# The third gate and up tile of a SwiGLU feed-forward, as two full products or as seven block products

## The chip, the core and the metric

The kernel runs on one core of a Trainium2 chip. The metric is the device time of one execution in microseconds (us), the median of several. Five engines run their own instruction queues side by side and wait for each other by semaphores: TensorE (PE; its weight loads are shown as PEld), VectorE (DVE), ScalarE (ACT), GpSimd (POOL) and SyncE (SP), which here issues the DMA transfers. Every engine takes its instructions in the order in which the program lists them.

## The reference

Two layers of an encoder trunk on a sequence of 512 positions with model width 1024, in float32. Each layer is a half-step feed-forward, a token mixing (windowed attention beside dilated attention), and a second half-step feed-forward. Only the feed-forward matters here:

```
h = modulate(rmsnorm(x, norm), shift, scale)
gate, up = split(h @ wi, 2)          # wi: 1024 x 5632, so 2 x 22 tiles of 128 columns
x = x + 0.5 * g * ((silu(gate) * up) @ wo)
```

There are four feed-forwards, two per layer. The columns of `wi` are taken as 22 pairs of tiles, f0 to f21: the gate tile f and the up tile f, 128 columns each.

## The kernel before, in words

**Tiles and splitting.** Activations lie transposed: 128 features on the partitions, 512 positions along the row, eight such tiles (k = 0 to 7) for the 1024 features. TensorE multiplies in a format that keeps fewer bits than float32, so each operand is split into a high part (rounded by ACT) and a low part (the rest, subtracted by DVE), and each product is three matmuls: high by high, low by high, high by low (`mm3`, L224 to L228; `prod`, L485 to L490).

**A full tile.** A flat gate or up tile of 128 columns is eight k, three matmuls each, of 512 positions: 24 matmuls of 128x512. A pair f made flat is 48 of them (L573 to L581). Its two weights are loaded and split by `emit_chunk` (L139): for each weight an ACT copy `hi` and a DVE subtraction `lo` (L157, L158).

**A pair by block products.** In three of the four feed-forwards (all but the first one of layer 0, `wino = l + sub > 0`, L441), a pair f may be made in one go by the seven products of Strassen's scheme in its Winograd form (`pair`, L475): the two weights of 1024 rows by 128 columns side by side are a 2 by 2 matrix of blocks, the activation is cut at feature 512 and at position 256 into four blocks, and seven products of blocks with four k each stand in for eight. That is 7 x 4 x 3 = 84 matmuls of 128x256. Which pairs are made so is told by

```
def paired(l, sub, f):                       # L105
    return l + sub > 0 and f >= PLAIN        # PLAIN = 3, L25
flat = 2 * min(n, max(0, PLAIN - f0)) if wino else 2 * n     # L572: tiles of this third that stay flat
```

The weights' side of it is `emit_pair` (L164): besides the splits it forms sums and differences of weight blocks. On DVE these are four operations of 128x512 (L191, L193, L198, L200: `ta` and `raw`), three low parts of 128x1024 and one of 128x512 (L188: three `lo` and `l4`); on ACT the high parts (L185, L199).

The activations' side is `sums(k)` (L452), once per feed-forward for k = 0 to 3: on DVE four sums of halves of `t` (L457 to L460), on ACT one high part `sh` of 128x1024 (L463), on DVE one low part `sl` of 128x1024 (L464). Every pair by block products reads all four `sh` and `sl`.

**The order of a feed-forward.** The 22 pairs go in thirds of 7, 7 and 8. The first third starts with `group` (L371): four flat tiles (gate and up of f0 and f1), each in two halves of 256 positions, since the norm of the second half of the positions comes later. Behind each of the four tiles, `sums(k)` is called for one k (L567), `take` (L552) makes the SwiGLU product of a finished gate and up (silu L559 on ACT, product L560 on DVE, split L471 and L472), and `ahead` (L217) emits the next weights. Then come the flat tiles that are left (before: f2), then the block products (before: f3 to f6), then the output tiles of this third (`out_tiles`, L403). `ahead` emits a block pair early only when at most one flat weight is waiting; further pairs are emitted piece by piece inside `pair` (the generator `more`, advanced by `conv`, L498).

**What sets the order on an engine.** The program is recorded in this order, and a scheduler then lists the instructions of each engine with its own costs for each; the list is fixed when the program is built. So the place of an instruction in its engine's list can move by more than the code shows.

The three feed-forwards with block products are called A (second of layer 0), B (first of layer 1) and C (second of layer 1) below.

Of the kernel before, what the change touches and what calls it, by code (L numbers as in the profile page):

```python
# [21 lines left out]
HS = 256  # L22
NF = 22
THIRDS = ((0, 7), (7, 7), (14, 8))
PLAIN = 3  # L25
EPS = 1e-6
TWO_PI = 6.283185307179586
PI_2 = 1.5707963267948966
# [40 lines left out]
def tile_trunk(ctx: ExitStack, tc: tile.TileContext, xT, c, positions, adaT, cols, sink, wi1, wo1,  # L69
# [35 lines left out]
    def paired(l, sub, f):  # L105
        return l + sub > 0 and f >= PLAIN

# [330 lines left out]
    def ffn(l, sub, norm, pool, step, start=None, final=None, mod=None):  # L438
# [109 lines left out]
        for ti, (f0, n) in enumerate(THIRDS):  # L548
# [15 lines left out]
            if ti == 0:  # L564
                for p in (start() if start else group(norm, gs, sh, 4)):
# [4 lines left out]
                    if start:  # L570
                        step()
            flat = 2 * min(n, max(0, PLAIN - f0)) if wino else 2 * n  # L572
            for _ in range(done, flat):  # L573
# [618 lines left out]
```

## Time and profile before

| | us |
|---|---|
| median of 3 runs | 1941.79 (1940.43 to 1943.55) |
| profiled execution, its own time | 1941.13 |
| span of that execution, first to last instruction | 1939.4 |
| PE busy | 1903.8 (98%) |
| DVE busy | 1516.0 (78%) |
| ACT busy | 941.6 (49%) |
| PE on the chain that ended last | 90% |
| mean granted clock of TensorE | 0.994 |

Matmuls overlap in the records: one of 128x256 is shown with 0.28 us, but the next one may start 0.12 us after it. What a stretch of matmuls takes is therefore read from start to start. The same holds on DVE and ACT, where an operation's record reaches some hundredths of a microsecond into the next one.

### The profile page before, as it was taken

How to read it: one execution, taken by the hardware profiler on the slowest of the kernel's cores; microseconds unless marked ns; L12 is line 12 of the kernel's file. 1: busy time of each engine (PE TensorE's matmuls, PEld its weight loads, DVE VectorE, ACT ScalarE, POOL GpSimd, SP SyncE). 2: the span in 40 equal slices, each digit the busy share in tenths (PEclk: the TensorE clock that was granted, in tenths of full speed). 3: DMA queues.
4: the chain of work that ended last, by engine and by line, in shares of the span. 5: the costliest groups of instructions: out<-in, count | busy, mean ns of one | idle time of the engine just before them, and what ended most of it. 6: DMA issues, size and time to landing. Idle time of an engine off the chain costs nothing.

```text
span 1939.4 us, 30969 instructions
## 1 busy us (share of the span) xinstructions
PE 1903.8 (98%) x12000; PEld 1711.2 (88%) x12000; DVE 1516.0 (78%) x2653; ACT 941.6 (49%) x1782; POOL 85.5 (4%) x63
## 2 busy tenths in 40 slices
PE   7999999999999999999999999999999999999998
PEld 5788888898778999989999898999887799898998
DVE  8967484477888989899688898867778889686873
ACT  5422222246675554536445363644567656363552
POOL 2000000011210000000000000000211000000000
PEclk8999999999999999999999999999999999999999
DMA  8778384245422255464424545342543113233231
GB/s 298 282 255 308 126 304 137 76 129 139 118 55 66 77 164 195 142 209 129 142 66 152 196 144 161 109 131 83 153 116 99 44 57 111 86 106 123 87 110 44
DMA packets 84677, 267.95 MB, mean 138 GB/s; under 512 B 10673, under 2 KB 13361, under 8 KB 84530
## 3 DMA queue, kind: packets, MB, share of 16 engines
q1 hardware_dynamic: 84530, 265.98, 42.6%
q8 instruction: 94, 1.54, 0.3%
q14 instruction: 53, 0.43, 0.1%
HBM read 244.97 MB, written 2.10 MB: 127 GB/s over the span
## 4 chain that ended last, share of the span: by engine, by line
PE 90%; DVE 5%; ACT 2%; DMA 2%; issue 1%; SPq 0%; POOL 0%; DVEq 0%; ACTq 0%; POOLq 0%
PE mm L226 17%; PE mm L227 17%; PE mm L228 17%; PE mm L488 10%; PE mm L489 10%; PE mm L490 10%; PE ptr L732 2%; PE po L739 1%; PE po L740 1%; PE s L698 1%; PE s L699 1%; DVE araw L320 1%; DMA araw<-in_adaT_dram 1%; PE mm L661 1%; PE mm L663 1%
## 5 line engine op out<-in xcount | busy, mean ns | idle before, releaser
L157 ACT ACTIVATE hi<-raw 128x512 fp32r<-128x512 f32 (+5 forms) x253 | 215.7, 866 | 310.2 <-PE mm L228 224.2
L158 DVE TENSOR_TENSOR lo<-raw,hi 128x512 fp32r<-128x512 f32 (+5 forms) x253 | 259.2, 1037 | 88.6 <-ACT hi L157 87.6
L226 PE MATMUL mm<-hh,hi 128*128 128x512 f32 (+1 forms) x864 | 307.7, 357 | 6.9 <-ACT hh L298 6.6
L228 PE MATMUL mm<-hl,hi 128*128 128x512 f32 (+1 forms) x864 | 303.1, 355 | 2.8 <-DVE hl L299 2.8
L227 PE MATMUL mm<-hh,lo 128*128 128x512 f32 (+1 forms) x864 | 305.8, 355 | 0.0
L227 PE MATMUL mm<-gh,lo 128*128 128x512 f32 (+1 forms) x832 | 297.0, 357 | 0.0
L226 PE MATMUL mm<-gh,hi 128*128 128x512 f32 (+1 forms) x832 | 296.8, 357 | 0.0
L228 PE MATMUL mm<-gl,hi 128*128 128x512 f32 (+1 forms) x832 | 296.5, 356 | 0.0
L488 PE MATMUL mm<-sh,hi 128*128 128x256 f32 x912 | 260.0, 285 | 0.3 <-ACT sc L518 0.3
L489 PE MATMUL mm<-sh,lo 128*128 128x256 f32 x912 | 258.1, 283 | 0.0
L490 PE MATMUL mm<-sl,hi 128*128 128x256 f32 x912 | 258.0, 283 | 0.0
L185 ACT ACTIVATE hi<-raw 128x512 fp32r<-128x512 f32 x228 | 132.0, 623 | 140.3 <-issue 73.6
L396 DVE SCALAR_TENSOR_TENSOR x<-mm,fin,x 128x512 f32<-128x512 f32 (+1 forms) x156 | 101.4, 653 | 115.7 <-PE mm L228 115.2
L226 PEld LDWEIGHTS mm<-hh,hi 128*128 128x128 f32 x864 | 164.6, 191 | 29.7 <-ACT hh L298 8.1
L228 PEld LDWEIGHTS mm<-hl,hi 128*128 128x128 f32 x864 | 163.2, 190 | 25.9 <-DVE hl L299 4.7
L227 PEld LDWEIGHTS mm<-hh,lo 128*128 128x128 f32 x864 | 164.4, 190 | 20.7 <-DVE lo L1004 0.3
L228 PEld LDWEIGHTS mm<-gl,hi 128*128 128x128 f32 x832 | 157.2, 189 | 22.7
L227 PEld LDWEIGHTS mm<-gh,lo 128*128 128x128 f32 x832 | 157.2, 189 | 22.3
L226 PEld LDWEIGHTS mm<-gh,hi 128*128 128x128 f32 x832 | 157.2, 189 | 22.2
L488 PEld LDWEIGHTS mm<-sh,hi 128*128 128x128 f32 x912 | 174.0, 191 | 0.7 <-ACT sc L518 0.6
L489 PEld LDWEIGHTS mm<-sh,lo 128*128 128x128 f32 x912 | 174.2, 191 | 0.0
L490 PEld LDWEIGHTS mm<-sl,hi 128*128 128x128 f32 x912 | 174.1, 191 | 0.0
(185 smaller groups left out, 4017.1 us busy)
## 6 DMA issues: line engine op xcount, KB each, us to landing
raw<-in_wi_dram SPq DMA_DIRECT2D x171, 512.0 KB, 3.7
araw<-in_adaT_dram SPq DMA_DIRECT2D x144, 512.0 KB, 4.6
raw<-in_wo_dram SPq DMA_DIRECT2D x64, 448.0 KB, 3.8
raw<-in_wo_dram SPq DMA_DIRECT2D x32, 512.0 KB, 3.6
raw<-in_wqk_dram SPq DMA_DIRECT2D x26, 512.0 KB, 3.7
raw<-in_w_out_dram SPq DMA_DIRECT2D x16, 512.0 KB, 3.7
kh<-qh SPq DMA_DIRECT2D x40, 128.0 KB, 2.3
kl<-t SPq DMA_DIRECT2D x40, 128.0 KB, 2.3
```

What stands on the lines that cost most here:

```text
L157: A.activation(hi[:, sl], raw[:, sl], AF.Copy)
L158: V.tensor_tensor(lo[:, sl], raw[:, sl], hi.bitcast(F32)[:, sl], op=ALU.subtract)
L185: A.activation(d, r, AF.Copy)
L226: T.matmul(ps, wh, X[0][:, s], start=start, stop=False)
L227: T.matmul(ps, wl, X[0][:, s], start=False, stop=False)
L228: T.matmul(ps, wh, X[1][:, s], start=False, stop=stop)
L320: return V.tensor_tensor_reduce(out=raw, in0=raw, in1=by, scale=1.0, scalar=0.0, op0=ALU.mult, op1=ALU.add, accum_out=mod[:, l, ch, k:k + ...
L396: ins = V.scalar_tensor_tensor(x[:, m, s], ps[:, s], gate[:, m:m + 1], x[:, m, s], op0=ALU.mult, op1=ALU.add).ins
L488: T.matmul(ps, wh, xh, start=start and k == 0, stop=False, skip_group_check=True)
L489: T.matmul(ps, wl, xh, start=False, stop=False, skip_group_check=True)
L490: T.matmul(ps, wh, xl, start=False, stop=stop and k == 3, skip_group_check=True)
L732: T.transpose(p[:, j * 128:j * 128 + 128], self.sm[qt][:, c0:c0 + 128], ident)
```

## The change

`PLAIN` goes from 3 to 2, so in A, B and C the pair f2, the first one behind `group`, is made by block products too. Nothing else in the code is touched.

```diff
 THIRDS = ((0, 7), (7, 7), (14, 8))
-PLAIN = 3
+PLAIN = 2
```

In A, B and C each, 48 matmuls of 128x512 are gone and 84 of 128x256 are new. The weights of f2 go through `emit_pair` instead of twice `emit_chunk`: the same two transfers of 512 KB, four DVE subtractions of 128x512 less, and the eight DVE operations of a block pair more. The product and the split of a finished f2 (L560, L472) become the five DVE operations L524, L530, L532, L540 and L544.

On DVE, in A, this is what stands behind the last sum of k = 0 (L460) before the change, up to the last sum of k = 1 (L460 again); `lo<-raw,hi` at L158 is the low part of f2's two flat weights, `sl` the low part of the sums:

```order
L460 SCALAR_TENSOR_TENSOR sf<-t,fin,sf 128x256
L158 TENSOR_TENSOR lo<-raw,hi 128x512 x4
L464 TENSOR_TENSOR sl<-sf,sh 128x1024
L457 SCALAR_TENSOR_TENSOR sf<-t,both 128x256
L459 TENSOR_TENSOR sf<-t 128x256
L458 SCALAR_TENSOR_TENSOR sf<-t,fin,sf 128x256
L560 TENSOR_TENSOR sg<-sg,mm 128x512
L460 SCALAR_TENSOR_TENSOR sf<-t,fin,sf 128x256
```

And with the change, from the same instruction to the first sum of k = 1; the rows between are the block pair f2's weights, with `sl` of k = 0 among them:

```order
L460 SCALAR_TENSOR_TENSOR sf<-t,fin,sf 128x256
L191 TENSOR_TENSOR ta<-raw 128x512
L188 TENSOR_TENSOR lo<-raw,hi 128x1024
L193 TENSOR_TENSOR ta<-ta,raw 128x512
L464 TENSOR_TENSOR sl<-sf,sh 128x1024
L198 TENSOR_TENSOR raw<-raw,ta 128x512
L200 TENSOR_TENSOR raw<-raw 128x512
L188 TENSOR_TENSOR lo<-ta,hi 128x1024
L188 TENSOR_TENSOR l_6116<-raw,h_6115 128x512
L188 TENSOR_TENSOR lo<-raw,hi 128x1024
L457 SCALAR_TENSOR_TENSOR sf<-t,both 128x256
```

The sums of k = 1, 2 and 3 stand behind the whole weight work of f2. In A and C the list from L457 of k = 1 to the last `sl` is the same as before, word for word. In B two of the weight operations (`L191` and the first `lo`) stand some rows earlier, where three of the four `lo` of the flat f2 stood before; the other six stand behind L460 as here.

On PE, in A, this is the last of f2's flat matmuls before the change, and the first of f3's block products behind it:

```order
L226 MATMUL mm_6286<-hh7_5828,hi_6113 128x512
L227 MATMUL mm_6286<-hh7_5828,lo_6114 128x512
L228 MATMUL mm_6286<-hl7_5829,hi_6113 128x512
L488 MATMUL mm_6318<-hh4_5822,hi_6262 128x256
L489 MATMUL mm_6318<-hh4_5822,lo_6265 128x256
```

With the change, f2's block products follow `group` at once. Two of its seven products (24 matmuls) read the plain activations `hh`, `hl`; then come the rows below, with `sh_6100`, `sh_6161`, `sh_6201` the sums of k = 0, 1, 2, `sl_...` their low parts, and `mm_6371` already belonging to f3:

```order
L490 MATMUL mm_6245<-hl3_5821,hi_6108 128x256
L488 MATMUL mm_6246<-sh_6100,hi_6109 128x256
L489 MATMUL mm_6246<-sh_6100,lo_6112 128x256
L490 MATMUL mm_6246<-sl_6101,hi_6109 128x256
L488 MATMUL mm_6371<-hh4_5822,hi_6265 128x256
L488 MATMUL mm_6246<-sh_6161,hi_6109 128x256
L489 MATMUL mm_6246<-sh_6161,lo_6112 128x256
L490 MATMUL mm_6246<-sl_6162,hi_6109 128x256
L488 MATMUL mm_6246<-sh_6201,hi_6109 128x256
L489 MATMUL mm_6246<-sh_6201,lo_6112 128x256
L490 MATMUL mm_6246<-sl_6202,hi_6109 128x256
```

So the first readers of the sums have moved from behind the flat f2 to the 25th matmul behind `group`. The first reader of k = 3's low part (`sl_6235`) is the 49th matmul behind `group`; what stands ahead of it are f2's first two products, its sums of k = 0 to 2 in two products, four matmuls of `sh` of k = 3, and two early matmuls of f3. B and C have the same list on PE but for one matmul's place.

## Rows read from the trace of the kernel before

**Rows 1.** The page, busy time of each engine: share of the span, instructions.

```profile
PE 1903.8 (98%) x12000; PEld 1711.2 (88%) x12000; DVE 1516.0 (78%) x2653; ACT 941.6 (49%) x1782; POOL 85.5 (4%) x63
```

**Rows 2.** Waits of PE, whole run: total us, times, longest us.

```profile
PE mm L488 <- ACT sc L518: 0.3, 1, 0.3
```

**Rows 3.** Timeline of PE in A: start us, us, instruction.

```profile
661.54 0.40 PE L226 MATMUL mm<-hh,hi 128*128 128x512 f32 x1
...
672.44 0.28 PE L488 MATMUL mm<-hh,hi 128*128 128x256 f32 x1
...
682.52 0.28 PE L488 MATMUL mm<-hh,hi 128*128 128x256 f32 x1
```

**Rows 4.** Timeline of DVE in A, behind the first sums.

```profile
652.98 0.49 DVE L460 SCALAR_TENSOR_TENSOR sf<-t,fin,sf 128x256 f32<-128x256 f32 x1
653.38 2.50 DVE L158 TENSOR_TENSOR lo<-raw,hi 128x512 fp32r<-128x512 f32 x4
655.79 1.23 DVE L464 TENSOR_TENSOR sl<-sf,sh 128x1024 fp32r<-128x1024 f32 x1
656.92 0.48 DVE L457 SCALAR_TENSOR_TENSOR sf<-t,both 128x256 f32<-128x256 f32 x1
657.32 0.42 DVE L459 TENSOR_TENSOR sf<-t 128x256 f32<-128x256 f32 x1
657.65 0.49 DVE L458 SCALAR_TENSOR_TENSOR sf<-t,fin,sf 128x256 f32<-128x256 f32 x1
...
660.00 0.69 DVE L472 TENSOR_TENSOR gl<-sg,gh 128x512 fp32r<-128x512 f32 x1 [0.47 <-ACT gh L471]
...
667.34 1.23 DVE L464 TENSOR_TENSOR sl<-sf,sh 128x1024 fp32r<-128x1024 f32 x1
```

**Rows 5.** Timeline of DVE in A, the weights of a block pair.

```profile
668.49 0.69 DVE L193 TENSOR_TENSOR ta<-ta,raw 128x512 f32<-128x512 f32 x1
669.09 1.22 DVE L188 TENSOR_TENSOR lo<-raw,hi 128x1024 fp32r<-128x1024 f32 x1
670.22 0.69 DVE L200 TENSOR_TENSOR raw<-raw 128x512 f32<-128x512 f32 x1
```

**Rows 6.** Timeline of ACT in A: the silu of f1's gate.

```profile
658.86 0.60 ACT L559 ACTIVATE sg<-mm 128x512 f32<-128x512 f32 x1 [2.94 <-PE mm L228]
```

**Rows 7.** Timeline of DVE in B, behind the first sums.

```profile
1001.76 0.48 DVE L460 SCALAR_TENSOR_TENSOR sf<-t,fin,sf 128x256 f32<-128x256 f32 x1
1002.15 0.69 DVE L158 TENSOR_TENSOR lo<-raw,hi 128x512 fp32r<-128x512 f32 x1
```

**Rows 8.** Timeline of PE in B, the first matmul of the flat f2.

```profile
1010.07 0.40 PE L226 MATMUL mm<-hh,hi 128*128 128x512 f32 x1
```

**Rows 9.** Timeline of DVE in C, behind the first sums.

```profile
1595.54 2.50 DVE L158 TENSOR_TENSOR lo<-raw,hi 128x512 fp32r<-128x512 f32 x4
```

**Rows 10.** Timeline of PE in C, the first matmul of the flat f2.

```profile
1603.69 0.40 PE L226 MATMUL mm<-hh,hi 128*128 128x512 f32 x1
```

**Rows 11.** Timeline of PE behind a wait, elsewhere.

```profile
613.71 0.50 PE L226 MATMUL mm<-yah,hi 128*128 128x512 f32 x1 [1.72 <-ACT yah L801]
614.05 0.40 PE L227 MATMUL mm<-yah,lo 128*128 128x512 f32 x1
```

**Rows 12.** Windows with PE: stretch, length, PE busy (matmuls), granted clock, DMA share, GB/s.

```profile
13.00:14.00 1.00, 0.28 (x2) 1.00 1.05 345
16.00:17.00 1.00, 0.20 (x2) 0.71 0.99 406
26.00:27.00 1.00, 1.00 (x5) 0.67 1.04 401
46.00:54.00 8.00, 5.40 (x23) 1.00 0.92 351
611.00:614.00 3.00, 1.28 (x8) 1.00 0.25 97
```

**Rows 13.** Windows with all engines, end of B's first third: PE, PEld, DVE, ACT, POOL.

```profile
1051.00:1061.00 10.00, 10.00 (x86) 10.00 (x85) 6.69 (x10) 5.15 (x8) 0.00 (x0) 1.00 0.76 242
```

## The prediction

> **What bounds the kernel now.** I read the page first: PE is busy 98% of the span and DVE 78% [rows 1]. An average over stages decides nothing, so the waits of PE came next. The block products (L488 to L490) wait once in the whole run, for 0.3 us [rows 2]: in A, B and C PE never stands still behind `group`, and its own matmuls set the time there. The timeline of PE gives their price. In A the flat f2 begins at 661.54 and f3's block products at 672.44, f4's at 682.52 [rows 3]: a flat pair takes 10.90 us (48 matmuls, 0.227 each), a block pair 10.08 us (84 matmuls, 0.120 each). The timeline of DVE at the same place shows what PE's timeline hides. From 652.98 on DVE works through the sums with hardly a gap, and the low part of the last one (L464 of k = 3) ends at 667.34 + 1.23 = 668.57 [rows 4], which is 7 us after `group` has ended on PE. Nobody waits for it today, since PE has the flat f2 to do until 672.44. The flat pair is the cover under which the sums are made, and the change takes it away.
>
> **The change, part by part.**
>
> *Fewer columns on PE.* In each of A, B and C, 10.90 us of flat matmuls give way to 10.08 us of block products: -0.82 us, three times -2.5 us. The rows price a matmul of 256 columns at 0.120 us, more than half of 0.227. The Trainium skill (TensorE: Matmul & The Clock Gate, "Wait — 56ns, not 53.3ns?") gives a start-to-start time of the columns at 2.4 GHz plus about 2.5 ns, which makes 0.109 and 0.216 us, and a gain of 1.2 us for each of the three. The trace has dearer matmuls [rows 3], so it decides; by the page's figures the sum would come out 1.1 us lower.
>
> *More work on DVE ahead of the sums, in A.* Behind the sums of k = 0 stand today the four low parts of the flat f2, from 653.38 to 655.79 = 2.41 us [rows 4]. In their place come f2's eight weight operations: five of 128x512 at 0.60 us (669.09 - 668.49) and three of 128x1024 at 1.13 us (670.22 - 669.09) [rows 5], together 6.4 us, or 4.0 us more. One of them, the third low part, needs a high part that ACT makes only behind the silu of f1's gate, which waits for PE until 658.86 and takes 0.60 [rows 6]; with 0.6 us for the copy itself (my estimate, as long as the silu of the same size) it is there at 660.0, where DVE would have begun at 659.8: 0.2 us more. So L457 of k = 1, at 656.92 today [rows 4], comes at about 661.1. From there on DVE's list is today's word for word, and today it holds one gap, 0.47 us at 660.00 for ACT [rows 4], of which I drop 0.4, since f1's silu no longer stands in its way. The last low part then ends at 668.57 + 4.2 - 0.4 = 672.3.
>
> *Earlier need on PE, in A.* f2's block products begin at 661.54 in place of its flat ones. The first 24 matmuls read what is long there. The 49th is the first to read the low part of k = 3, and without a wait it would start at 661.54 + 48 x 0.120 = 667.3. It can't before 672.3: 5.0 us of waiting, spread over the chain k = 1 to 3. By the same sum DVE and ACT give the low part of k = 1 at 665.9 (0.8 us late), the high part of k = 2 at 667.7 (1.6 more), its low part at 669.5 (1.5 more), the rest before the last one. A resumed PE also loses something: behind a wait its second matmul came 0.34 us after the first, where 0.227 is the pace [rows 11], so 0.1 us; the restarts ahead of the 49th matmul lie inside the 5.0 us, three at or behind it (the last part of k = 3, f3's first weights, a copy by ACT) add 0.3. Together +5.3 us. PE is strictly in order, and the two matmuls of f3 that stand among these rows are too few to fill anything.
>
> *Not given back.* Queued behind PE's waits is all that follows in the feed-forward; as PE waited for nothing there [rows 2], a late start of f4 is a late end. f4 starts at 661.54 + 168 x 0.120 + 5.3 = 687.0 against 682.52 [rows 3]: +4.5 us in A.
>
> *C* repeats A: its DVE list is at the same operation at 1595.54 [rows 9], 942.16 us after A's 653.38, and PE at its flat f2 at 1603.69 [rows 10], 942.15 after 661.54. +4.5 us.
>
> *B* is milder. Three of f2's four flat low parts stand earlier in the list and make room there for two of the weight operations, so that six are left behind the first sums, with the low part of k = 0 among them. From 1002.15 [rows 7] these are four operations at 0.60 (three before that low part, one behind) and three of 1.13: 5.8 us, and L457 of k = 1 begins at 1007.95. From there to the end of the last low part it is as in A 11.2 us (672.3 - 661.1): 1019.15. PE begins f2 at 1010.07 [rows 8] and would be at its 49th matmul at 1015.83. Wait 3.3 us, 0.3 behind it, less 0.8: +2.8 us.
>
> *What lies beside other work.* DVE has some 5 us more to do in each first third (6.4 - 2.4 for the weights, about 1.3 for five combining operations in place of two). By the third's end it has room: in B from 1051 to 1061 it was busy 6.69 of 10 us while PE was full [rows 13]. Without that room it would cost up to 5 us each time; I take nothing. ACT, POOL and the two transfers of 512 KB are the same work at almost the same place, and the few transfers that change places on SP lie where PE waits for none.
>
> *Sum.* 4.5 + 2.8 + 4.5 = +11.8 us on the profiled execution's 1941.13 us: 1952.9. The median of the runs shown lies 0.7 us higher, so 1953.
>
> **The rivals.**
>
> *The products pay, the sums are in time.* PE takes its 0.82 us in each feed-forward and waits no more than today: 1941.8 - 2.5 = 1939.3, not slower. For it speaks that the block pairs wait for nothing now [rows 2]. It would need the last low part 4.2 us earlier than I have it in A, at about 668.1: from there the wait eats less than 0.82. Against it speaks that DVE runs without a gap from before the weight operations to the last low part, so nothing can bring it forward, and that its list is fixed.
>
> *Half of it is given back.* If PE's later pairs have hidden waits of other kinds, or DVE's list moves on faster than its neighbours suggest, the waits shrink to 2 to 3 us each: 1944 to 1949. Only the 0.3 us of [rows 2] is there to be given back, and the durations in the rows repeat to a hundredth.
>
> *TensorE's clock falls in the gaps.* At the start of the run PE was busy 0.28 us from 13 to 14 us, then hardly at all, and the granted clock went from 1.00 to 0.71 in the microsecond from 16 and came back in the one from 26 [rows 12]: some 10 us at 1.2 in place of 2.4 GHz. In A and C, PE will do only six matmuls between 664.9 and 669.5, in four pieces. If that is too little, up to 8 us of block products behind the gaps run at half speed and cost 4 us each in A and C: 1961. Against it: from 46 to 54 us PE was busy 5.4 of 8 us and the clock stayed at 1.00, and so it did around the wait of 1.72 us [rows 11], from 611 to 614 [rows 12]. The Trainium skill (TensorE: Matmul & The Clock Gate, "What's actually happening") says that the throttled state is the default and activity releases it; by that rule the gaps are a risk, and the first two of [rows 12] agree, but nothing in this trace shows gaps as dense as these.
>
> **How the numbers follow.** My forecast, all waits as computed and full clock: 78%, 1953, of its own range 1950 to 1956, since the unknown terms are small: the restarts (0 to 0.6 each time), the 0.4 and 0.2 us around ACT, and B's start. The clock: 12%, 1957 to 1965. Half given back: 6%. No wait: 4%. For 8 in 10 the range is 1949 to 1960: it holds my forecast's range, all but the top of the clock's and the edge of the third case. A measurement of this kernel tells about 0.2%, or 3.9 us, from no change. The forecast, the clock and most of the half are slower by more: 0.94. The case without waits lies at -0.13%, inside: it and the low end of the half make 0.04. A faster run would need more than all three savings: 0.02.
>
> **What would show it.** In the profile after, PE's waits must have new rows for L488 on ACT's `sh` (L463) and L490 on DVE's `sl` (L464), together some 3 to 4 us in each of A and C and 2 to 3 in B (the records of 0.28 us hide 0.16 of each wait), and hardly a row for f4 and later. The last L464 in A ends near 672.3 with DVE gapless ahead of it, f4's first matmul starts near 687.0, and 168 matmuls of 256 columns lie between `group`'s end and there. I am wrong if these waits are missing, if the distance from `group`'s end to f4 in A is under 22 us, if the granted clock falls below 1 there, or if DVE falls behind in the third's output tiles, which would add waits of L226 there.

## The result, and the profile after

The changed kernel takes 1960.64 us (median of four runs, 1957.55 to 1962.84) against 1942.28 us in the same job (1940.43 to 1943.55): ratio 1.0090, 95% interval 1.0073 to 1.0107, slower by 14 to 21 us. The forecast was 1953, the range 1949 to 1960. The median lies 0.6 us above the range; taken by the ratio from 1941.79, where the forecast started, it is 1959.3, inside by 0.7. The direction and the waits came as forecast; the size is larger, and TensorE's clock, which the forecast took as full, has a part in it. The profiled execution took 1958.53 us, 17.4 more than before's, and its span is 1956.4 us, 17.0 more.

The page, busy time by engine, answers to [rows 1]:

```profile
PE 1910.4 (98%) x12108; PEld 1720.2 (88%) x12108; DVE 1532.9 (78%) x2674; ACT 949.9 (49%) x1800; POOL 85.6 (4%) x63
```

PE's share has not moved. An average shows nothing of a loss of 17 us that sits in three places. The waits of PE (total us, times, longest us) show it; against [rows 2] the block products have two new rows, 9.2 us in eight waits:

```profile
PE mm L490 <- DVE sl L464: 5.1, 5, 1.3
PE mm L488 <- ACT sh L463: 4.1, 3, 1.4
PE mm L488 <- ACT sc L518: 0.2, 1, 0.2
```

The timeline of PE in A, from the first matmul of f2 (`group`'s end, as it is called below) to the first of f4, answers to [rows 3]:

```profile
664.10 0.28 PE L488 MATMUL mm<-hh,hi 128*128 128x256 f32 x1
...
667.58 0.28 PE L489 MATMUL mm<-sh,lo 128*128 128x256 f32 x1
668.50 0.39 PE L490 MATMUL mm<-sl,hi 128*128 128x256 f32 x1 [0.64 <-DVE sl L464]
670.32 0.39 PE L488 MATMUL mm<-sh,hi 128*128 128x256 f32 x1 [1.43 <-ACT sh L463]
670.55 0.28 PE L489 MATMUL mm<-sh,lo 128*128 128x256 f32 x1
672.09 0.58 PE L490 MATMUL mm<-sl,hi 128*128 128x256 f32 x1 [1.27 <-DVE sl L464]
672.57 0.58 PE L488 MATMUL mm<-sh,hi 128*128 128x256 f32 x1
...
673.38 0.41 PE L488 MATMUL mm<-sh,hi 128*128 128x256 f32 x1
673.59 0.41 PE L489 MATMUL mm<-sh,lo 128*128 128x256 f32 x1
...
675.50 0.28 PE L490 MATMUL mm<-sl,hi 128*128 128x256 f32 x1
...
690.12 0.28 PE L488 MATMUL mm<-hh,hi 128*128 128x256 f32 x1
```

Three gaps stand ahead of the low part of k = 1 and of the high and the low part of k = 2. From start to start they lose 0.8, 1.7 and 1.4 us, where the working had 0.8, 1.6 and 1.5. The line at 675.50 is the 49th matmul, the first to read the low part of k = 3; the fourth wait of the working, ahead of it, is not there. Behind the third gap the matmuls follow each other at 0.21 us and not at 0.120. The windows with PE (stretch, length, PE busy, granted clock, DMA share, GB/s) say why:

```profile
670.00:671.00 1.00, 0.50 (x2) 1.00 0.00 0
671.00:672.00 1.00, 0.00 (x0) 0.90 0.00 0
672.00:673.00 1.00, 0.91 (x3) 0.50 0.00 0
674.00:675.00 1.00, 1.00 (x7) 0.50 0.08 16
675.00:676.00 1.00, 1.00 (x10) 0.90 0.32 33
676.00:677.00 1.00, 1.00 (x11) 1.00 0.82 246
```

PE had begun three matmuls since 667.7 when the granted clock went to 0.50 (1.2 GHz) at 671.8; it came back at 675.2. The same happened in C, not in B. The third rival of the prediction, which had 12%, is part of the answer.

DVE's last low part in A answers to [rows 4], where it ended 7.03 us behind `group`'s end (668.57 - 661.54). Here it ends 673.56 + 1.23 - 664.10 = 10.69 us behind it; the forecast said 672.3 - 661.54 = 10.76. The 49th matmul starts 11.40 us behind `group`'s end, so PE, at half clock, came 0.7 us later than the operand that it was to wait for.

```profile
673.56 1.23 DVE L464 TENSOR_TENSOR sl<-sf,sh 128x1024 fp32r<-128x1024 f32 x1
```

One measure serves for all that follows: the distance from `group`'s end to f4's first matmul, read from PE's timeline in each phase of each profile. A phase that starts late for another reason does not change it. "Lows" are low parts of the sums. Us:

| kernel | A | B | C | sum, over before's 63.0 | runs, ratio to before [95%] |
|---|---|---|---|---|---|
| before | 20.98 | 21.06 | 20.98 | 0 | 1 |
| forecast for the change | 25.5 | 23.9 | 25.5 | +11.8 | 1.0058 |
| changed | 26.02 | 24.36 | 26.37 | +13.7 | 1.0090 [1.0073, 1.0107] |
| e1 changed, again | 27.19 | 24.38 | 27.14 | +15.7 | 1.0090 [1.0076, 1.0104] |
| e2 only B changed | 20.98 | 25.26 | 20.98 | +4.2 | 1.0023 [1.0015, 1.0032] |
| e3 before, two lows more | 20.98 | 20.98 | 20.98 | -0.1 | 0.9997 [0.9988, 1.0006] |
| e4 changed, two lows more | 28.49 | 27.37 | 28.70 | +21.5 | 1.0129 [1.0114, 1.0145] |
| e5 changed, sums ahead | 22.96 | 22.16 | 22.98 | +5.1 | 1.0034 [1.0021, 1.0046] |
| e6 e5 and two lows on GpSimd | 26.14 | 24.31 | 26.09 | +13.5 | 1.0084 [1.0072, 1.0097] |
| e7 changed, waits filled | 25.45 | 25.26 | 25.47 | +13.2 | 1.0082 [1.0068, 1.0096] |
| e8 before, f3 flat too | 21.79 | 21.79 | 21.79 | +2.4 | 1.0020 [1.0011, 1.0028] |
| e9 before, again | 20.98 | 21.06 | 20.98 | 0 | 1.0004 [0.9995, 1.0013] |
| e10 before, start edited | 20.98 | 21.06 | 20.98 | 0 | 0.9986 [0.9977, 0.9995] |
| e11 changed, start edited | 27.48 | 25.09 | 27.26 | +16.8 | 1.0077 [1.0063, 1.0091] |

Of the first profile's 17.0 us, 13.7 lie in the three phases. Most of the rest (2.6 us) was lost before A began: `group` ended at 664.10 against 661.54, in a part of the program that the change does not touch: up to 600 us the instructions in the two traces are, engine by engine, the same in the same order.

### The profile page after: what moved, and what is told of

Same layout as the page of the kernel before. It is cut to its first block, busy times and chain, and to the rows that moved or that the text cites. A ratio compares the mean times of both kernels' runs of the same rounds, so it can differ in the third digit from the quotient of the medians.

```text
span 1956.4 us, 31234 instructions
## 1 busy us (share of the span) xinstructions
PE 1910.4 (98%) x12108; PEld 1720.2 (88%) x12108; DVE 1532.9 (78%) x2674; ACT 949.9 (49%) x1800; POOL 85.6 (4%) x63
## 4 chain that ended last, share of the span: by engine, by line
PE 87%; DVE 6%; ACT 2%; DMA 2%; issue 1%; POOL 0%; SPq 0%; DVEq 0%; ACTq 0%; POOLq 0%
PE mm L226 16%; PE mm L228 16%; PE mm L227 16%; PE mm L488 10%; PE mm L490 10%; PE mm L489 10%; PE ptr L732 2%; PE po L739 1%; PE po L740 1%; PE s L698 1%; DMA araw<-in_adaT_dram 1%; PE s L699 1%; PE mm L661 1%; PE mm L663 1%; PE mm L662 1%
## 5 line engine op out<-in xcount | busy, mean ns | idle before, releaser
L157 ACT ACTIVATE hi<-raw 128x1024 fp32r<-128x1024 f32 (+5 forms) x241 | 208.3, 878 | 309.4 <-PE mm L228 222.8
L158 DVE TENSOR_TENSOR lo<-raw,hi 128x1024 fp32r<-128x1024 f32 (+5 forms) x241 | 251.3, 1053 | 85.6 <-ACT hi L157 84.4
L226 PE MATMUL mm<-hh,hi 128*128 128x512 f32 (+1 forms) x816 | 289.7, 356 | 8.2 <-ACT hh L298 8.2
L227 PE MATMUL mm<-hh,lo 128*128 128x512 f32 (+1 forms) x816 | 288.1, 354 | 0.0
L228 PE MATMUL mm<-hl,hi 128*128 128x512 f32 (+1 forms) x816 | 284.8, 354 | 1.7 <-DVE hl L299 1.7
L488 PE MATMUL mm<-sh,hi 128*128 128x256 f32 x960 | 275.7, 287 | 4.5 <-ACT sh L463 4.1
L490 PE MATMUL mm<-sl,hi 128*128 128x256 f32 x960 | 273.2, 285 | 5.2 <-DVE sl L464 5.1
L489 PE MATMUL mm<-sh,lo 128*128 128x256 f32 x960 | 272.6, 284 | 0.0
L488 PEld LDWEIGHTS mm<-sh,hi 128*128 128x128 f32 x960 | 184.8, 192 | 6.7 <-ACT sh L463 4.7
L489 PEld LDWEIGHTS mm<-sh,lo 128*128 128x128 f32 x960 | 185.0, 193 | 0.0
```

What stands on the lines that cost most here:

```text
L157: A.activation(hi[:, sl], raw[:, sl], AF.Copy)
L158: V.tensor_tensor(lo[:, sl], raw[:, sl], hi.bitcast(F32)[:, sl], op=ALU.subtract)
L226: T.matmul(ps, wh, X[0][:, s], start=start, stop=False)
L227: T.matmul(ps, wl, X[0][:, s], start=False, stop=False)
L228: T.matmul(ps, wh, X[1][:, s], start=False, stop=stop)
L488: T.matmul(ps, wh, xh, start=start and k == 0, stop=False, skip_group_check=True)
```

## The experiments

**Theory 1:** the sums come late on DVE, whose list is in order and has nothing to spare there, and PE waits for the last of them, since the flat f2 no longer covers them. **Rivals:** the clock makes the price and not DVE; DVE's added work costs wherever it stands; the loss lies elsewhere in the program.

### e1: the changed kernel again, and e9: the kernel before again

No edit.

> The changed kernel again, unchanged. Of the 17.0 us by which its first profile was longer than that of before, 13.7 lay between group's end and f4 of the three phases (A 5.0, B 3.3, C 5.4) and 3.6 elsewhere (2.6 ahead of A, of which 2.0 came from one stretch of half clock at 54 to 60 us, and 1.0 between B and C). Theory 1 (the sums are late, and the rest is chance from one execution to the next): the three phases repeat within 0.3 us each, 13.4 to 14.4 in all, and the 3.6 us come out otherwise, anywhere from 0 to 5. Theory 2 (the change costs elsewhere too): the 2.0 us at 54 to 60 us and the 1.0 between B and C are there again. Median against before: +15 to +19 us.

Measured: +15.7 us in the phases, outside the 13.4 to 14.4 that was expected. B repeats to 0.02 us, A and C came out 1.2 and 0.8 longer. The stretch of half clock near 55 us, theory 2's sign, was there again (55.6 to 62.4); e9 tells whether it belongs to the change. DVE's last low part again ended 10.7 us behind `group`'s end (673.70 against 663.02), and the three gaps are the same to 0.1 us. What differs is the clock, lower for longer:

```profile
668.00:669.00 1.00, 0.00 (x0) 1.00 0.00 0
669.00:670.00 1.00, 0.50 (x2) 0.97 0.00 0
670.00:671.00 1.00, 0.00 (x0) 0.50 0.00 0
676.00:677.00 1.00, 1.00 (x7) 0.61 0.49 197
677.00:678.00 1.00, 1.00 (x10) 1.00 0.00 0
```

Here it fell at 669.9, 3.3 us behind the first wait's beginning, and stayed down for 6.8 us; in the first profile it fell 4.1 us behind it, for 3.4 us. So for the same waits the price of the clock varies between executions.

> The kernel before again, unchanged, for a second look at what lies outside the three phases. Theory 1 (what the changed kernel lost there is chance of the start): group's end in A comes anywhere from 661 to 665 us, with a stretch of half clock near 55 us in some executions; group's end to f4 21.0 us in all three phases. Rival (the start of the kernel before is free of that stretch by its program): 661.5 within 0.3, and no half clock between 30 and 500 us, as in its first profile.

Measured: the phases are those of before, and `group` ends in A at 664.51, 3.0 us later than in before's first profile. The rival (a start that is free of half clock by its program) has fallen. The windows with PE at the start of e9:

```profile
53.00:54.00 1.00, 0.00 (x0) 1.00 0.87 258
54.00:55.00 1.00, 0.00 (x0) 0.62 0.80 283
55.00:60.00 5.00, 4.96 (x12) 0.50 0.58 202
61.00:62.00 1.00, 1.00 (x5) 0.97 0.00 0
```

The kernel before has this stretch too, behind a wait of 3.70 us as long as the changed kernel's. Of the eleven profiles whose start is not edited, eight have it, with and without the change. So the stretch is not the change's doing. This execution took 1944.59 us, before's first 1941.13.

### e2: only B

```diff
-PLAIN = 3
+PLAIN = {(0, 2): 3, (1, 0): 3, (1, 2): 3}
+PLAIN[(1, 0)] = 2
...
-        return l + sub > 0 and f >= PLAIN
+        return l + sub > 0 and f >= PLAIN[l, sub]
```

(The lines between are left out, and so is the same key where `flat` is worked out. The keys are A, B and C.)

> f2 of B alone as block products, A and C as before. Theory 1 (each phase pays by itself): group's end to f4 is 24.4 us in B and 20.98 in A and C, no stretch of clock under 1 in A or C, and the time is 3.3 us over before (1.0 to 5.5 with what varies between executions). Rival (the loss of one phase is carried by the others, or the weights' queue is shifted for the whole run): B differs from 24.4 by over 0.5 us, or A or C from 20.98.

Measured: A and C are those of before to 0.01 us, with the clock at full there. A phase pays for itself and for no other. B is 25.26, 0.9 over the changed kernel's: this time the granted clock fell in B too, from 1020.6 to 1024.0. PE's waits there (1.24 and 1.27 us) and the end of the last low part (9.59 us behind `group`'s end) are those of the changed kernel's B, so the distance missed its bound of 0.5 by the clock, and not by a coupling.

### e3 and e4: two low parts made twice, with and without the cover

```diff
-            V.tensor_tensor(lo, f, h.bitcast(F32), op=ALU.subtract)
+            for _ in range(2 if k in (1, 2) else 1): V.tensor_tensor(lo, f, h.bitcast(F32), op=ALU.subtract)
```

e3 is this edit in the kernel before, e4 in the changed one.

> The kernel before (f2 flat) with the low parts of the sums of k = 1 and k = 2 made twice: 2 x 1.14 = 2.28 us more for DVE ahead of the last low part, in each of A, B and C. Theory 1 (the flat f2 is a cover of 8 us for the sums, and of 2.25 us for f3's first weights behind them): at most 0.1 us each, group's end to f4 stays at 21.0 to 21.2 us in all three, and the time is that of before, within 1 us. Rival (DVE's added work costs wherever it stands, since DVE falls behind for the rest of the third): +2.3 us each, +6.8 in all.

> The changed kernel (f2 as block products) with the same two low parts made twice, 2.28 us more for DVE in each of A, B and C. Theory 1 (no cover is left, PE waits for the last low part and DVE is the path): group's end to f4 grows by 2.0 to 2.5 us in each phase, to 28.2, 26.6 and 28.6 us, in all +6 to +7.5 us over the changed kernel in the same job. Rival (the clock, and not DVE, makes the price; DVE has slack behind the first wait): under 1 us each, under 3 in all.

Measured: behind the flat f2 the added work costs nothing (20.98 us in all three phases, ratio 0.9997). Without the cover it costs 1.0129 against 1.0090, 0.39% of 1942.7, or 7.6 us, where 6 to 7.5 was expected; by the phases 5.8 us over e1, 7.8 over the first profile. The last low part on DVE and f4's first matmul in A, first in e3 (`group`'s end at 661.39), then in e4 (662.66):

```profile
668.86 1.22 DVE L464 TENSOR_TENSOR sl<-sf,sh 128x1024 fp32r<-128x1024 f32 x1
682.37 0.28 PE L488 MATMUL mm<-hh,hi 128*128 128x256 f32 x1
```

```profile
673.79 1.22 DVE L464 TENSOR_TENSOR sl<-sf,sh 128x1024 fp32r<-128x1024 f32 x1
691.15 0.28 PE L488 MATMUL mm<-hh,hi 128*128 128x256 f32 x1
```

In A the last low part moved by 1.66 us in both kernels, from 7.03 to 8.69 behind `group`'s end in e3 and from 10.69 to 12.35 in e4. That is not the full 2.28, since f3's first weight operation (L191, 0.60 us), which stood ahead of it, came to stand behind it. (In B of e3 it moved by the full 2.28, at no cost.) 3 x 1.66 = 5.0 us of e4's loss are that part's; the clock fell in all three phases of e4. The same work, once free and once on the path: the cover is shown, and the rival that DVE's work costs wherever it stands has fallen.

### e5: all four sums ahead of most of f2's weights

```diff
-                    if wino:
-                        sums(done)
+                    if wino and done == 0:
+                        sums(0)
+                        late = emit_pair()
+                        for _ in range(3):
+                            next(late)
+                        for k in range(1, 4):
+                            sums(k)
+                        for _ in late:
+                            pass
```

> f2 as block products as in the changed kernel, the same operations, but all four sums stand behind f2's first low part on DVE, and f2's other five weight operations among and behind them. Theory 1 (DVE's order sets the price; summed along its new list, the second low part of the weights, needed 3.1 us behind group's end, is there 4.6 us behind it in A and C and 5.7 in B, the last low part of the sums just in time): one wait of 1.5 us in A and C, 2.6 in B, and 0.4 to 0.6 at f3. Group's end to f4: 22.3, 23.5, 22.3 us (changed kernel 26.0 to 27.2, 24.4, 26.4 to 27.1), in all 5 us over before, no half clock in A and C. Rival (the amount of DVE work ahead of f2's end sets it, in whatever order): 24 to 27 us each, as in the changed kernel, 14 to 16 over before.

Measured: 22.96, 22.16 and 22.98, in all 5.1 us over before where 5 was expected, and no half clock in A, B or C. The split was off: A and C are 0.7 dearer, B 1.3 cheaper than summed. No operation was taken away, only the order changed, and 8.6 of 13.7 us are gone. PE's waits in A (rows of the block products, 600 to 700 us) are small and each has another source:

```profile
PE mm L489 <- DVE lo L188: 0.7, 1, 0.7
PE mm L488 <- ACT sc L521: 0.4, 1, 0.4
PE mm L488 <- ACT sc L510: 0.4, 1, 0.4
```

### e6: e5, with two of the low parts on GpSimd

```diff
-            V.tensor_tensor(lo, f, h.bitcast(F32), op=ALU.subtract)
+            (G if k in (1, 2) else V).tensor_tensor(lo, f, h.bitcast(F32), op=ALU.subtract)
```

> As the one with the sums ahead, and the low parts of the sums of k = 1 and k = 2 made by GpSimd (2.4 us each by its five 128x1024 operations at the start, beside DVE's 1.14). Theory 1: DVE gives the second low part of the weights 2.0 us behind group's end in A and C, 3.0 in B, both before its need; the last low part of the sums comes 5.3 and 6.3 us behind it for a need near 5.2. Group's end to f4: 20.3 to 20.7 us in A and C, 21.3 in B; in all 0 to 1.5 us less than before, and the time within 0.2% of it. Rival (GpSimd's work slows DVE beside it, or its own low parts come late): a new wait for GpSimd's sl of over 1 us a phase, or DVE's operations longer than 0.60 and 1.14, and 22 us or more.

Measured: 26.14, 24.31, 26.09, as dear as the changed kernel; the clock fell in A and C, for 3.4 us each. The expectation failed by its rival, and in two ways. GpSimd's timeline in A, then DVE's in A and in B:

```profile
663.75 5.31 POOL L464 TENSOR_TENSOR sl<-sf,sh 128x1024 fp32r<-128x1024 f32 x2 [88.86 <-ACT sh L463]
```

```profile
663.78 0.68 DVE L200 TENSOR_TENSOR raw<-raw 128x512 f32<-128x512 f32 x1
666.77 2.58 DVE L457 SCALAR_TENSOR_TENSOR sf<-t,both 128x256 f32<-128x256 f32 x1 [2.31 <-POOL sl L464]
669.27 0.41 DVE L459 TENSOR_TENSOR sf<-t 128x256 f32<-128x256 f32 x1
...
1020.54 2.62 DVE L460 SCALAR_TENSOR_TENSOR sf<-t,fin,sf 128x256 f32<-128x256 f32 x1
...
1024.43 2.63 DVE L458 SCALAR_TENSOR_TENSOR sf<-t,fin,sf 128x256 f32<-128x256 f32 x1
```

First a wait that I had overlooked: the sum of k = 3 is written into the buffer of k = 1, and DVE stands 2.31 us until GpSimd has read it. Then an operation that lasts 0.47 us elsewhere lasts 2.58 to 2.63, to the end of GpSimd's. The Trainium skill (SBUF — State Buffer, "Who interferes with whom") says that a DVE instruction with two inputs in SBUF contends with a GpSimd instruction that reads SBUF, that the ports the two share are an exclusive lock, and that the order of issue decides which of them blocks. These rows agree: the DVE operations that began behind GpSimd's took 2.58 to 2.63 us.

### e7: the waits filled with matmuls

```diff
-                    T.matmul(ps, wl, xh, start=False, stop=False, skip_group_check=True)
+                    T.matmul(ps, wl, xh, start=False, stop=False, skip_group_check=True); filler((0, fill[0], fill[2], 0)[k], wl, xh)
-                    T.matmul(ps, wh, xl, start=False, stop=stop and k == 3, skip_group_check=True)
+                    T.matmul(ps, wh, xl, start=False, stop=stop and k == 3, skip_group_check=True); filler((0, fill[1], 0, 0)[k], wh, xl)
```

The rest of the edit is left out: `filler` issues that many matmuls of 256 columns into a spare buffer; `fill` is (5, 11, 9) for f2's third product in A and C and nought elsewhere, and the 11 stand behind the low part of k = 1.

> The changed kernel with 5, 11 and 9 matmuls of 256 columns, whose results nobody reads, put into PE's three waits in A and C (0.6, 1.3 and 1.1 us of 0.8, 1.7 and 1.4); B stays as it is. Theory 1 with the clock as a part (PE falls to 1.2 GHz in A and C because it stands still there, and this costs what group's end to f4 has above DVE's last low part): no stretch under 1 in A and C, and 25.3 to 25.7 us there in place of 26.0 to 27.2; in all 1 to 3.5 us less than the changed kernel. B 24.4 as before. Rival (the clock falls for another reason, or its fall lies under the waits and costs nothing): the same 26 to 27 us.

Measured: 25.45 and 25.47 in A and C, inside the 25.3 to 25.7 that was expected. The timeline of PE in A, from `group`'s end at 663.56 (the fillers, the one wait that the profile still shows, the first reader of the low part of k = 3, f4's first matmul), then the windows:

```profile
667.16 0.76 PE L111 MATMUL fill<-sh,lo 128*128 128x256 f32 x5
668.18 1.46 PE L111 MATMUL fill<-sl,hi 128*128 128x256 f32 x11
670.12 1.24 PE L111 MATMUL fill<-sh,lo 128*128 128x256 f32 x9
671.55 0.38 PE L495 MATMUL mm<-sl,hi 128*128 128x256 f32 x1 [0.19 <-DVE sl L469]
...
674.30 0.39 PE L495 MATMUL mm<-sl,hi 128*128 128x256 f32 x1
...
689.01 0.28 PE L493 MATMUL mm<-hh,hi 128*128 128x256 f32 x1
```

```profile
666.00:670.00 4.00, 3.83 (x30) 1.00 0.22 87
670.00:674.00 4.00, 3.72 (x26) 1.00 0.00 0
674.00:678.00 4.00, 3.89 (x30) 1.00 0.43 131
```

25 matmuls that compute nothing, and the phase is 0.6 to 2.0 us shorter than in the three profiles without them (26.02, 27.19, 27.48). The reader of the low part of k = 3 now starts 10.74 us behind `group`'s end, 0.05 behind that part; in the first profile it started at 11.40. That A and C lost their clock to the gaps, and what it costs, is shown by these phases. In B, left as it was, the clock fell this time (from 1025.3 to 1028.8), and B took 25.26. By the times the gain is 1.0082 against 1.0090, within both intervals, so the times alone show no gain.

### e8: f3 flat too

```diff
-PLAIN = 3
+PLAIN = 4
```

> The other way: f3 is made flat as well in the three phases (four flat pairs in place of before's three). Theory 1 (three pairs are cover enough, one more flat pair costs 10.90 - 10.08 us and frees no wait): group's end to f4 is 21.80 us in each phase, 0.82 more than before, 2.5 us in all: 0.13% slower. Rival (before still hides waits for the sums or for f3's weights): under 0.4 us each, or faster than before.

Measured: 21.79 in all three phases, 0.81 (A, C) and 0.73 (B) more than before. The saving of a pair is what the rows had, once the cover is there: before has cover enough, and no wait is hidden in it. The time is 0.20% over before, where 0.13% was expected, inside the interval.

### e10 and e11: the start without the last GpSimd product

```diff
-BY_POOL = (1, 3, 4, 6, 7)
+BY_POOL = (1, 3, 4, 6)
```

e10 is this edit in the kernel before, e11 in the changed one.

> The kernel before with the last of GpSimd's five products at the start (k = 7) made by DVE instead (1.21 us as one of its reductions). In every profile so far, one DVE operation between 46 and 49 us lasts 2.6 to 3.5 us in place of 0.41 to 1.31, as long as GpSimd's product beside it. Theory (DVE is held up by GpSimd's operation, and PE's wait of 2 to 3.7 us behind it lets the clock fall): that operation takes its usual time, DVE is about 1 us further at 52 us, and the time is 0 to 3 us less than before. Rival (the start waits for its transfers): the same time, within 0.1%.

> The changed kernel with the same edit of the start. Theory: no stretch of half clock between 50 and 65 us; 1 to 4 us less than the changed kernel, the three phases as before with it (26 to 27, 24.4, 26 to 27 us), in all 13 to 16 us over the kernel before with this edit. Rival: no difference from the changed kernel, 18 us over before.

Measured: e10 is 0.14% faster than before (0.05 to 0.23%), 2.7 us, and the fastest version of all. DVE in e9, the unedited kernel, then GpSimd in it, then the same DVE operation in e10:

```profile
47.59 2.97 DVE L1004 TENSOR_TENSOR lo<-raw,hi 128x256 fp32r<-128x256 f32 x2
```

```profile
47.77 2.51 POOL L317 TENSOR_TENSOR araw<-araw,cs 128x1024 f32<-128x1024 f32 x1 [3.48 <-DVE hl L299]
```

```profile
48.04 0.75 DVE L1004 TENSOR_TENSOR lo<-raw,hi 128x256 fp32r<-128x256 f32 x2
```

Without GpSimd's operation beside them the two take 0.75 us and not 2.97, and in this execution no half clock follows (windows of e10):

```profile
50.00:55.00 5.00, 3.94 (x17) 1.00 1.00 393
55.00:60.00 5.00, 4.71 (x21) 1.00 0.13 49
```

That the long operation is what brings the clock down is not shown. Among the eleven profiles whose start is not edited, before, e3 and e4 have a long operation of DVE there and no half clock near 55 us; e7 and e8 have the half clock (3.4 us, from 55.95 and from 53.66 on) though the two operations took 0.75 us. Those two are also exceptions to the expectation's "every profile so far". The gain in time is shown, its cause is open.

With the edit the changed kernel gains as much (1957.62 against 1960.3 us) and stays 18.0 us over e10. Its phases are 16.8 over before's (27.48, 25.09, 27.26), above the 13 to 16 that was expected, since the clock fell in all three, B too. Neither profile has half clock from 50 to 65 us. So the difference between the two kernels is the same with a start that is free of that stretch.

## Why the prediction was right, and where its size was off

*The cover.* Right. e3 and e4 show it from both sides, and the last low part came where the list put it: 10.69 us behind `group`'s end in A and 10.68 in C, forecast 10.76. In B it came at 9.58, forecast 9.08: the half microsecond that B is dearer than summed. The sum for B ran DVE's list through without a gap, but DVE stands 0.40 us ahead of the low part of k = 0, for ACT's high part:

```profile
1012.61 1.22 DVE L464 TENSOR_TENSOR sl<-sf,sh 128x1024 fp32r<-128x1024 f32 x1 [0.40 <-ACT sh L463]
```

The kernel before has the same wait there, of 0.54 us at 1004.50.

*The saving of 0.82 us a pair.* Right: 0.73 to 0.81 in e8.

*The waits.* Right. In A PE's two new rows hold 3.3 us, forecast 3 to 4, eight waits in all three phases; where the clock fell, the wait ahead of the last low part was taken up by the slow matmuls. f4 and later wait for hardly anything, as forecast. With the clock held up (e7) A and C measure 25.45 and 25.47, where 20.98 + 4.5 = 25.5 was forecast. With B at full clock (24.36) the sum is +12.3 us, forecast +11.8.

*DVE's further 5 us a third, taken at nothing.* Right: between f4 of A and 960 us, past the end of its feed-forward, PE's one wait is the 0.2 us of L518 (in e1 there are 0.9 us, of L510 and L518). From f4 of C to the end of the run it is 314.7 us before and 314.6 with the change.

*The clock.* This is the step that failed. The sum of 11.8 us holds nothing for it, and a granted clock under 1 in A stood among the prediction's own signs of being wrong. "TensorE's clock falls in the gaps" stood at 12% as a rival that excludes the forecast; it came in A and C in every profile in which PE had these waits unfilled, and in B in some, beside the forecast waits and not in their place. My evidence against it was one wait of 1.72 us and a stretch with 5.4 of 8 us busy [rows 12], neither of which is three waits within 5 us. Its price was mis-sized the other way: not 4 us in each of A and C, but 0.6, 1.7 and 2.0 us in A in the first profile, e1 and e11 (26.02, 27.19 and 27.48 less 25.45), and 0.7 to 0.9 us in B where it fell there. A matmul at 1.2 GHz takes 0.21 us in place of 0.120, but at first PE does at half speed what it would otherwise wait for: the first profile's low clock ended 0.4 us after the last low part had landed. So the phases cost 13.7 to 16.8 us, 11.8 of them forecast. That the range still held the result, by the 0.7 us of the ratio, is luck: its top was said to hold all but the top of the clock's case, 1957 to 1965, but it leaves out that case's own 1961.

*What is still open.* By the ratio the kernels differ by 17.5 us (14 to 21), by the phases of three profiles 13.7, 15.7 and 16.8. Profiles show one execution each. In the first pair the span's 17.0 us are 13.7 in the phases, 2.6 ahead of A and 0.8 elsewhere; in e10 and e11 its 17.5 us are 16.8, 0.9 (`group` ends in A at 660.29 and 661.20) and -0.2. The clock's low stretches in the mixers, which both kernels have, differ in length from one execution to the next. Most of what is lost ahead of A comes in the kernel before as well (e9), by a list of instructions that is the same. Whether the change adds to it is not settled: `group` ended in A between 660.9 and 664.5 us in the five profiles with A as before and the start unedited, and between 662.7 and 664.8 in the six with the change in A; and a further stretch of half clock, of 3.4 us near 35 us, stands in e4, e5, e6 and e11 alone, all with the change in A.

## What to carry to other kernels

Before work is taken off the busiest engine, ask who uses its time as cover: here 0.82 us less on PE laid bare 5 us of DVE. Price the waits that follow as a row of gaps and not one by one: here three of 0.8 to 1.7 us within 5 us brought the clock down in A and C, where one of 1.72 us at 612 had not. And when an in-order list is what is late, its order can be worth more than its length: in e5 the order alone took back 8.6 of 13.7 us. A free engine was no help where its work held up the late one and shared a buffer with it (e6).

## What the hardware showed that I had not expected

- The same program with the same waits (0.1 us apart) lost the clock in A for 3.4 us in one execution and for 6.8 in the next. In B, with the same two waits of 1.24 and 1.27 us, it fell in e2, e7 and e11, but not in the first profile and e1.
- 25 matmuls that compute nothing, 3.0 us of work, made a phase 0.6 to 2.0 us shorter (e7).
- DVE's operations of two inputs took 2.58 to 2.63 us in place of 0.47 beside one GpSimd operation (e6), and a pair of them 2.97 in place of 0.75 (e9). The profile shows this as a long operation, and not as a wait.
